# Dealing a projection's matmuls into a recurrence: fewer pieces per preparation, another order of groups, an earlier substitution, a shared tile

## The chip, the cores and the metric

The kernel runs on one core of one Trainium2 chip, as one launch. The metric is device time in microseconds (us). A core has a matmul engine (PE, TensorE), a vector engine (DVE), an activation engine (ACT), GpSimd (POOL) and a queue engine (SP) that issues its DMAs. Each engine works through its own instructions in the order in which they are written down for it; they wait for each other on semaphores.

## The reference

Two transformer blocks on 512 tokens of width 1024, in float32. The first (a hybrid layer: neighbourhood attention, gated linear attention, a convolutional feed-forward network) isn't touched by the change and takes the first 800 us. The second block is:

```
h = rms_norm(x); proj = h @ w_in                      # columns: q, k, v | RWKV columns | gates
attn = windowed_gqa(q, k, v)                           # window of 128, 8 query heads
zr = shift(proj[RWKV columns])                         # r, k, v, decay, rate, gate of the RWKV part
rw = rwkv7_time_mix(zr)                                # 8 heads of 64, forward and backward:
#   state = state * w_t + (state @ a_t) b_t^T + v_t k_t^T;   y_t = state @ r_t
x = x + (gates0 * (attn @ w_up_attn) + gates1 * (rw @ w_up_rwkv)) @ w_out
x = x + relu(rms_norm(x) @ w_ff1)^2 @ w_ff2
x = x + (p @ w_ple) * sigmoid(rms_norm(x) @ w_ple_gate)
```

## The kernel before, in words

The change lies in the method `block2`, in the stage in which the RWKV recurrence is worked out (about 800 to 1242 us of the profiled span). The eight heads are four **parts** of two heads, and the 512 tokens are eight chunks of 64, so that the recurrence becomes matrix work. A part p passes through these functions:

- `prep(p)` (L1060 to L1172): decay, rate and key vectors. PE makes `psw`, `pkn` and `pkr`, ACT and DVE make `kn` (L1096) out of them; here the generator yields the first time. Then, for direction d = 0 and d = 1: `pa`, `pcs` on PE, exponentials on ACT, `kd`, `a`, `u`, `BK`, `Z` on DVE (for d = 1 some of it on POOL), the matmuls `pP` of `Z` and `BK` (L1148), whose masked results `M` (L1151) are stored to DRAM as `scL` (L1157). It yields a second time after d = 0.
- `subst(p)` (L1174): two loads of `scL`, one into `LF` (512 KB, L1178) and one in two halves into `XH` (L1180), then 30 forward-substitution steps on DVE, two small instructions each (`sx` L1186, `XH` L1188), which invert the triangles of 32 rows.
- `finish(p)` (L1191): the result goes over DRAM (`scX`) into `M`, and PE joins the inverted blocks (`pax`, `pt`, `pg`) by way of the tile `AXt`.
- `pre(p)` (L1230), then `chain(p)` (L1258): eight dependent steps over the chunks (`pcb` on PE, `w`, `PV`, `S` on DVE, `W` on ACT), the outputs `pya` and `pyb`, their normalisation (`Z` at L1336, the tile called YT in the code), a yield, and what follows it (`pyt`, `pgt`, `rwd`).

**Pieces.** The projection `h @ w_in` is cut into column groups. Groups 2, 3, 4 are K, R, V of part 0, groups 5, 6, 7 those of part 1, then 8 to 10 and 11 to 13; groups 14 to 29 are the gates (tiles `gt`, stored as `gtd`); "qkv" is the projection for the attention. A group is 24 matmuls of 128x512, "qkv" 288 of 128x256. They need nothing of the recurrence, so they are dealt into it: `queue` (L1485) holds the order of the groups, and `pump(n)` writes the next n pieces into the program at that place (for "qkv" a piece is two matmuls). Groups 2 to 4 are worked out earlier. When a group of K, R or V is done, `cb_rk` and `shift` (L1027 to L1046) write it to `zk`, `zr` or `zv`; the tiles `zk` and `zr` have one buffer each, `zv` two. `need(p)` (L1504) pumps until K, R and V of part p are done. What is left of the queue after chain 3 is written out before the attention.

**Order.** The main loop (L1513 to L1539) writes: `prep(0)`, `need(1)`, `prep(1)`, `subst(0)`, 48 pieces, `finish(0)`, `pre(0)`; and for each p `chain(p)` up to its yield, `subst(p+1)`, `need(p+2)`, `prep(p+2)` up to its first yield, the rest of the chain, `prep(p+2)` up to its second yield, `finish(p+1)`, the rest of `prep(p+2)`, `pre(p+1)`. A scheduler then sets each engine's order; what stands where is shown in the section on the change.

I call **gap p** the time between the end of chain p's `pya`/`pyb` and the first `pcb` of chain p+1.

## Time and profile before

| | us |
|---|---|
| median of 3 runs | 1809.57 (1806.54 to 1810.01) |
| the profiled execution | 1813.19 |
| its span | 1811.4 |
| PE busy in it | 1697.5 |
| start of chain 0 (first `pcb`) | 935.2 |
| gap 0, chain 1, gap 1, chain 2 start at | 970.3, 1013.2, 1052.1, 1117.8 |
| gap 2, chain 3 start at, chain 3 ends at | 1157.1, 1196.8, 1230.0 |
| first matmul of the attention | 1241.85 |

The stages of the table are those that the prediction speaks of. In a timeline row the first number is the start within the span, the second the length, and in square brackets stands how long the engine had been idle and what ended it. The granted clock of PE is told as a share of its upper level of 2.4 GHz; its lower level is 1.2 GHz. A wide "busy" of PE includes matmuls at the lower clock.

### The profile page before, as it was taken

To read this page: it belongs to the slowest core of one execution; us is meant where nothing else is said; L and a number is where in the kernel's file an instruction comes from. 1 tells how busy PE (TensorE), PEld (TensorE's weight loads), DVE (VectorE), ACT (ScalarE), POOL (GpSimd) and SP (SyncE) were. 2 spreads that over 40 slices of the span, in tenths; PEclk is the share of its full clock that TensorE was granted. 3 is DMA by queue.
4 is the path that set the end of the run, shared out by engine and by line. 5 is a ranking of instruction groups with operands and counts; after the bars stand their busy time and mean duration, and the time that the engine had idled before them with its cause. 6 is when DMAs were issued, how large, how long until landed. Compare 5 with 4: busy or idle time off the path is not lost.

```text
span 1811.4 us, 31700 instructions
## 1 busy us (share of the span) xinstructions
PE 1697.5 (94%) x12168; PEld 1427.6 (79%) x12168; DVE 1127.3 (62%) x2375; ACT 780.4 (43%) x1526; POOL 215.7 (12%) x270
## 2 busy tenths in 40 slices
PE   8999998999999999888799898896899999999998
PEld 7888886889988999866676577764478888888887
DVE  5665776787742776867857674765665553355445
ACT  5453456764432445564234232334634442244333
POOL 1100121110000001363321212211000000000000
PEclk9899999999999999999899898897999999999999
DMA  5221223643333334632231212122054333333334
GB/s 170 52 60 48 61 78 113 178 143 99 88 96 97 89 93 139 170 113 62 72 89 45 88 48 67 47 68 70 1 186 146 99 94 99 94 95 98 93 99 129
DMA packets 116087, 170.89 MB, mean 94 GB/s; under 512 B 28839, under 2 KB 43439, under 8 KB 115936
## 3 DMA queue, kind: packets, MB, share of 16 engines
q1 hardware_dynamic: 115936, 168.87, 32.4%
q8 instruction: 96, 1.57, 0.4%
q14 instruction: 55, 0.45, 0.1%
HBM read 155.19 MB, written 13.63 MB: 93 GB/s over the span
## 4 chain that ended last, share of the span: by engine, by line
PE 42%; DVE 8%; DMA 3%; issue 2%; ACT 2%; SPq 1%; POOL 0%; ACTq 0%; DVEq 0%; POOLq 0%
PE ps_w_ff L251 20%; PE ps_w_in L268 5%; PE ps_w_out L251 2%; PE ps_w_ple_gate L251 2%; DMA XH<-scL 1%; PE ps_qkv L1366 1%; PE pP L1148 1%; PE ps_w_up_rwkv L251 1%; DVE sx L1186 1%; PE ps_w_up_attn L251 1%; DVE XH L1188 1%; PE po L1469 1%; DMA LF<-scL 1%; DVE BK L1137 1%; PE pcb L1281 1%
## 5 line engine op out<-in xcount | busy, mean ns | idle before, releaser
L203 DVE TENSOR_TENSOR wl_w_ff<-raw_w_ff,wh_w_ff 128x512 fp32r<-128x512 f32 x128 | 88.2, 689 | 129.8 <-ACT wh_w_ff L202 129.7
L202 ACT ACTIVATE wh_w_ff<-raw_w_ff 128x512 fp32r<-128x512 f32 x128 | 81.0, 632 | 192.2 <-PE ps_w_ff L251 183.4
L202 ACT ACTIVATE wh_w_in<-raw_w_in 128x512 fp32r<-128x512 f32 (+1 forms) x118 | 72.9, 622 | 116.2 <-PE ps_w_in L268 51.3
L203 POOL TENSOR_TENSOR wl_w_in<-raw_w_in,wh_w_in 128x512 fp32r<-128x512 f32 x60 | 81.1, 1354 | 196.7 <-ACT wh_w_in L202 117.4
L202 ACT ACTIVATE wh_w_ffn_in<-raw_w_ffn_in 128x512 fp32r<-128x512 f32 x96 | 60.0, 630 | 99.8 <-PE ps_w_ffn_in L251 88.1
L251 PE MATMUL ps_w_ff<-Yl,wh_w_ff 128*128 128x512 f32 x256 | 100.9, 394 | 0.0
L251 PE MATMUL ps_w_ff<-Yh,wh_w_ff 128*128 128x512 f32 x256 | 100.3, 392 | 0.0
L251 PE MATMUL ps_w_ff<-Yh,wl_w_ff 128*128 128x512 f32 x256 | 99.3, 388 | 0.0
L251 PE MATMUL ps_w_ffn_out<-Y_hi,wl_w_ffn_out 128*128 128x256 f32 (+1 forms) x256 | 83.5, 326 | 3.2 <-DVE wl_w_ffn_out L203 3.1
L251 PE MATMUL ps_w_ffn_out<-Y_hi,wh_w_ffn_out 128*128 128x256 f32 (+1 forms) x256 | 83.6, 326 | 0.0
L251 PE MATMUL ps_w_ffn_out<-Y_lo,wh_w_ffn_out 128*128 128x256 f32 (+1 forms) x256 | 83.3, 326 | 0.0
L203 DVE TENSOR_TENSOR wl_w_ffn_out<-raw_w_ffn_out,wh_w_ffn_out 128x512 fp32r<-128x512 f32 (+1 forms) x72 | 47.4, 663 | 48.2 <-ACT wh_w_ffn_out L202 47.8
L203 DVE TENSOR_TENSOR wl_w_ffn_in<-raw_w_ffn_in,wh_w_ffn_in 128x512 fp32r<-128x512 f32 x96 | 65.7, 689 | 17.0 <-ACT wh_w_ffn_in L202 16.0
L251 PE MATMUL ps_w_ffn_in<-fa_hi,wl_w_ffn_in 128*128 128x258 f32 x352 | 74.3, 285 | 2.0 <-DVE wl_w_ffn_in L203 2.0
L251 PE MATMUL ps_w_ffn_in<-fa_hi,wh_w_ffn_in 128*128 128x258 f32 x352 | 74.0, 284 | 1.7 <-ACT wh_w_ffn_in L202 1.7
L251 PE MATMUL ps_w_ffn_in<-fb_hi,wl_w_ffn_in 128*128 128x258 f32 x352 | 74.0, 284 | 0.2 <-DVE wl_w_ffn_in L203 0.2
L251 PE MATMUL ps_w_ffn_in<-fa_lo,wh_w_ffn_in 128*128 128x258 f32 x352 | 74.2, 284 | 0.0
L251 PE MATMUL ps_w_ffn_in<-fb_hi,wh_w_ffn_in 128*128 128x258 f32 x352 | 74.1, 285 | 0.0
L251 PE MATMUL ps_w_ffn_in<-fb_lo,wh_w_ffn_in 128*128 128x258 f32 x352 | 74.1, 285 | 0.0
L202 ACT ACTIVATE wh_w_ffn_out<-raw_w_ffn_out 128x512 fp32r<-128x512 f32 (+1 forms) x72 | 41.6, 582 | 61.9 <-PE ps_w_ffn_out L251 46.5
L251 PEld LDWEIGHTS ps_w_ffn_in<-fa_hi,wl_w_ffn_in 128*128 128x128 f32 x352 | 56.3, 191 | 2.4 <-DVE wl_w_ffn_in L203 2.4
L251 PEld LDWEIGHTS ps_w_ffn_in<-fa_hi,wh_w_ffn_in 128*128 128x128 f32 x352 | 56.1, 190 | 2.2 <-ACT wh_w_ffn_in L202 1.9
(675 smaller groups left out, 5172.5 us busy)
## 6 DMA issues: line engine op xcount, KB each, us to landing
raw_w_ff<-in_w_ff SPq DMA_DIRECT2D x128, 256.0 KB
raw_w_in<-in_w_in SPq DMA_DIRECT2D x116, 256.0 KB
raw_w_ffn_in<-in_w_ffn_in SPq DMA_DIRECT2D x96, 256.0 KB
raw_w_ffn_out<-in_w_ffn_out SPq DMA_DIRECT2D x40, 256.0 KB
raw_w_o<-in_w_o SPq DMA_DIRECT2D x32, 256.0 KB
raw_w_ffn_out<-in_w_ffn_out SPq DMA_DIRECT2D x32, 192.0 KB
gtd<-gt SPq DMA_DIRECT2D x16, 256.0 KB
g<-gtd SPq DMA_DIRECT2D x16, 256.0 KB
```

The costliest lines, as they stand in the source:

```text
L202: a = nc.scalar.activation(hi, src, AF.Copy)
L203: v = (eng or nc.vector).tensor_tensor(lo, src, hi, ALU.subtract)
L251: mm = nc.tensor.matmul(ps[si][:ncol, :s1 - s0], a[:, k, :], bk[:, s0:s1], start=(ks == k0 and k == 0 and pi == 0), stop=(ks + k == kend - ...
L268: nc.tensor.matmul(pw[:ncol, 0, :n], a[:, k, :], b[kk // 4][:, kk % 4, :n], start=(kk == 0 and pi == 0), stop=(kk == kend - 1 and pi == 2))
L1137: nc.vector.scalar_tensor_tensor(BK[H[e], :, O[e]], perm(a[H[e]], 64), -0.5, perm(iE[H[e]], 64), ALU.mult, ALU.mult)
L1148: nc.tensor.matmul(pps[e][:, i, :], BK[H[e], 4 * hf + i, :], Z[hf][H[e], i, :], start=True, stop=True)
L1186: nc.vector.tensor_tensor(sv, XH[:, 0:k, t:t + 1].to_broadcast([128, k, n]), LF[:, t % 2, t // 2:t // 2 + 1, t + 1:32].to_broadcast([128, ...
L1188: nc.vector.tensor_tensor(XH[:, 0:k, t + 1:32], XH[:, 0:k, t + 1:32], sv, ALU.add)
L1281: nc.tensor.matmul(pu[O[e], d, :], M[e][O[e], d, cd[d], 0:64], w[O[e], d, :], start=True, stop=True)
L1366: nc.tensor.matmul(pq[i][:, :256], l, r[:, k - ks, :], start=(k == 0 and n == 0 and i % 2 == 0), stop=(k == 7 and n == 2 and i % 2 == 1))
L1469: nc.tensor.matmul(po[own[g]], KVv[:, b0 + b, 128 + 64 * g:192 + 64 * g], PT[n % 2][:, g, b, :], start=b == 0, stop=b == nk - 1)
```

## The change

The order of the main loop becomes one loop over p (below). For p = 0, `need(5, 6)` pumps K and R of part 1 only, `subst(0)` follows the first third of `prep(1)`, and `finish(0)` comes between the two directions of `prep(1)`, with 24 pieces where it had 12; the block of 48 pieces is gone. The preparations of parts 2 and 3 deal 32 pieces each where they had 69. The queue names other groups first. `zk` has two buffers. The tile `AXt` of `finish`, which had a buffer of its own, now takes the buffer of `LF` (half of it), and that there is only one such buffer stays.

```diff
-                dct, nm, bf = ((Kt, "zk", 1), (R, "zr", 1), (V, "zv", 2))[j]
+                dct, nm, bf = ((Kt, "zk", 2), (R, "zr", 1), (V, "zv", 2))[j]
...
-            pump(4)
+            pump(2 if p else 4)
...
-            pump(8)
+            pump(4 if p else 8)
...
-                    pump((18, 15)[d] if len(Z) == 1 else 6)
+                    pump((8 if p else (18, 15)[d]) if len(Z) == 1 else 2 if p else 6)
...
-                    pump(4 if len(BKT) == 1 else 2)
+                    pump((4 if len(BKT) == 1 else 2) // (2 if p else 1))
...
-            AXt = rk.tile([128, 2, 8, 32], F32, tag="AX", name=f"AX{p}")
-            pump(12 if p == 0 else 6)
+            AXt = rk.tile([128, 2, 16, 32], F32, tag="LF", name=f"AX{p}").rearrange("p h m t -> p (h m t)")[:, :512].rearrange("p (d c t) -> p d c t", d=2, c=8)
+            pump(24 if p == 0 else 6)
...
-        queue = [5, 6, 7] + list(range(14, 19)) + [8, 9, 10] + list(range(19, 23)) + [11, 12, 13, 23, "qkv"] + list(range(24, 30))
+        queue = [5, 7, 14, 6, 15, 16, 8, 9, 17, 10, 18, 11, 12, 19, 13, "qkv"] + list(range(20, 30))
...
-        def need(p):
-            while not set(range(3 * p + 2, 3 * p + 5)) <= done | {2, 3, 4}:
+        def need(*gs):
+            while not set(gs) <= done | {2, 3, 4}:
                 pump(1)
...
         run(prep(0))
-        need(1)
-        run(prep(1))
-        XH = subst(0, pr[0][4])
-        pump(48)
-        finish(0, XH, pr[0][3])
-        x = pre(0, *pr[0][:4])
+        tail = iter(())
         for p in range(4):
-            ch = chain(p, *pr[p][:4], *x)
-            run(ch, 1)
-            nx = None
+            if p:
+                XH = subst(p, pr[p][4])
+            nx = iter(())
             if p < 3:
-                XH = subst(p + 1, pr[p + 1][4])
-            if p < 2:
-                need(p + 2)
-                nx = prep(p + 2)
+                need(3 * p + 5, 3 * p + 6)
+                nx = prep(p + 1)
                 run(nx, 1)
-            run(ch)
-            if p < 3:
-                if nx:
-                    run(nx, 1)
-                finish(p + 1, XH, pr[p + 1][3])
-                if nx:
-                    run(nx)
-                x = pre(p + 1, *pr[p + 1][:4])
+            if not p:
+                XH = subst(p, pr[p][4])
+            run(tail)
+            run(nx, 1)
+            finish(p, XH, pr[p][3])
+            run(nx)
+            need(3 * p + 4)
+            x = pre(p, *pr[p][:4])
+            tail = chain(p, *pr[p][:4], *x)
+            run(tail, 1)
+        run(tail)
```

How many pieces stand ahead of certain places in PE's order ("qkv" counted as two matmuls a piece):

| pieces written before | before | after |
|---|---|---|
| chain 0 starts / ends | 253 / 303 | 238 / 308 |
| chain 1 starts / ends | 360 / 423 | 333 / 383 |
| chain 2 starts / ends | 528 / 578 | 444 / 496 |
| chain 3 starts / ends | 639 / 703 | 567 / 629 |

The first place is DVE around the first step of substitution 0. A name like `kd10` is tile `kd` of part 1, direction 0; `sx01` is step 1 of part 0. Before:

```order
L1096 TENSOR_TENSOR kn1_10024<-kn1_10024,pkr1_10056 128x512
L1119 TENSOR_SCALAR kd10_10078<-a10_10068,kah_82,ka1_81 128x512
...
L1143 TENSOR_TENSOR Z101_10132<-zr1_9902,Er_9644 128x4x64
L1056 TENSOR_TENSOR gt1_10220<-ps_w_in_2_15_10106,rsh_75 128x512
L1186 TENSOR_TENSOR sx01_10314<-XH0_10310,LF0_10309 128x30
L1188 TENSOR_TENSOR XH0_10310<-XH0_10310,sx01_10314 128x30
L1186 TENSOR_TENSOR sx02_10317<-XH0_10310,LF0_10309 128x29
```

In the changed kernel the same place reads:

```order
L1096 TENSOR_TENSOR kn1_10065<-kn1_10065,pkr1_10085 128x512
L1186 TENSOR_TENSOR sx01_10096<-XH0_10092,LF0_10091 128x30
L1188 TENSOR_TENSOR XH0_10092<-XH0_10092,sx01_10096 128x30
...
L1186 TENSOR_TENSOR sx06_10111<-XH0_10092,LF0_10091 128x75
L1056 TENSOR_TENSOR gt1_10303<-ps_w_in_2_15_10041,rsh_75 128x512
L1188 TENSOR_TENSOR XH0_10092<-XH0_10092,sx06_10111 128x3x25
L1119 TENSOR_SCALAR kd10_10202<-a10_10192,kah_82,ka1_81 128x512
L1186 TENSOR_TENSOR sx07_10114<-XH0_10092,LF0_10091 128x96
```

The whole DVE work of direction 0 of preparation 1 (twelve instructions) has moved from ahead of `sx01` to behind its sixth step, and so has the tile `gt1`.

The second place is SP's queue around the load of `LF` for part 1; in the brackets stand the engines and DMA queues whose semaphores the load waits for. Before:

```order
L1203 DMA M01_9736<-scX0_10488 16x16x32 [waits DMAHW3_49]
L1178 DMA LF1_11103<-scL1_10065 128x1x1024 [waits DMAHW4_49]
L1180 DMA XH1_11104<-scL1_10065 64x512 [waits DMAHW5_49]
L1180 DMA XH1_11104<-scL1_10065 64x512 [waits DMAHW6_49]
L211 DMA raw_w_in_2_2555904_11235<-in_w_in_2 128x512 [waits DMAHW7_49,Pool_49]
```

And in the changed kernel:

```order
L1180 DMA XH1_11019<-scL1_10189 64x512 [waits DMAHW6_49,DMAHW2_49]
L1180 DMA XH1_11019<-scL1_10189 64x512 [waits DMAHW7_49,DMAHW3_49]
L211 DMA raw_w_in_2_1441792_11462<-in_w_in_2 128x512 [waits DMAHW4_49,Pool_49]
L1178 DMA LF1_11018<-scL1_10189 128x1x1024 [waits DMAHW5_49,DVE_49,PE_49]
L211 DMA raw_w_in_2_1507328_11634<-in_w_in_2 128x512 [waits Pool_49]
```

The load waits for DVE and PE now, since its buffer is that of `AX0`, which the matmuls `pg` of `finish(0)` (L1226) read last. `LF1`'s first reader, `sx11`, stands on DVE behind `w01`, the `w` of chain 0's step 1, in the changed kernel; before, it stood ahead of the chain's first step.

The third place is DVE at the first step of substitution 2, which runs beside chain 1; `w12` is the `w` of step 2 of chain 1. Before:

```order
L1277 TENSOR_TENSOR w12_11824<-pcb12_11819,W01_11685 128x128
...
L1277 TENSOR_TENSOR w13_11858<-pcb13_11853,W01_11685 128x128
L1042 TENSOR_TENSOR zs11_11881<-zt0_9641 128x512
L1186 TENSOR_TENSOR sx21_12126<-XH2_12122,LF2_12121 128x30
L1044 SCALAR_TENSOR_TENSOR zk3_11880<-zs11_11881,mu2_78,zk3_11880 128x512
```

And in the changed kernel:

```order
L1277 TENSOR_TENSOR w11_11648<-pcb11_11643,W01_11542 128x128
L1088 TENSOR_SCALAR knr3_12095<-pkn3_12090 128x8
...
L1277 TENSOR_TENSOR w12_11676<-pcb12_11671,W01_11542 128x128
L1096 TENSOR_TENSOR kn3_12084<-kn3_12084,pkr3_12104 128x512
L1186 TENSOR_TENSOR sx21_11978<-XH2_11974,LF2_11973 128x30
```

The step stands one chain step earlier, and the first third of preparation 3, which before came after chain 1 (`kn3` stood behind the last step of substitution 2), is now done inside chain 1; the first `Z` of part 3 stands behind step 21 of substitution 2. Substitution 3's first step, which stood behind one `w` of chain 2, now stands behind three.

## Rows read from the trace of the kernel before

**Rows 1.** page, section 1: busy us (share of the span) xinstructions, whole kernel

```profile
PE 1697.5 (94%) x12168; PEld 1427.6 (79%) x12168; DVE 1127.3 (62%) x2375; ACT 780.4 (43%) x1526; POOL 215.7 (12%) x270
```

**Rows 2.** busy time per engine by stretch; columns as its first line says

```profile
core 0: us, PE busy (x) PEld busy (x) DVE busy (x) ACT busy (x) POOL busy (x), PEclk, DMA share, GB/s
871.70:911.90 40.20, 34.94 (x166) 27.99 (x167) 35.14 (x80) 10.48 (x18) 14.67 (x12) 0.82 0.23 59
911.90:935.20 23.30, 22.25 (x329) 18.10 (x328) 9.70 (x14) 7.20 (x12) 3.98 (x4) 0.91 0.44 119
935.20:970.30 35.10, 34.34 (x448) 24.31 (x447) 27.73 (x94) 12.39 (x24) 6.51 (x5) 0.96 0.15 42
970.30:1013.20 42.90, 38.76 (x464) 29.78 (x457) 30.62 (x59) 17.33 (x29) 10.81 (x9) 0.92 0.25 65
1013.20:1052.10 38.90, 33.25 (x425) 22.04 (x424) 24.64 (x76) 8.12 (x18) 7.85 (x7) 0.91 0.26 77
1052.10:1117.80 65.70, 61.22 (x601) 51.11 (x600) 41.70 (x84) 23.83 (x43) 16.06 (x13) 0.90 0.22 56
1117.80:1157.10 39.30, 32.96 (x467) 27.49 (x466) 21.46 (x84) 9.15 (x21) 6.87 (x6) 0.87 0.16 51
```

**Rows 3.** DVE timeline: start us, us, line op out<-in, [idle before <-releaser]

```profile
871.71 0.19 DVE L1186 TENSOR_TENSOR sx<-XH,LF 128x30 f32<-128x30 f32 x1 [2.94 <-issue]
...
932.11 0.68 DVE L1016 COPY M<-pg 32x512 f32<-32x512 f32 x1 [2.94 <-PE pg L1226]
...
934.72 0.19 DVE L1186 TENSOR_TENSOR sx<-XH,LF 128x30 f32<-128x30 f32 x1
...
939.35 0.29 DVE L1277 TENSOR_TENSOR w<-pcb,W 128x128 f32<-128x128 f32 x1 [0.19 <-PE pcb L1275]
```

**Rows 4.** SP timeline (DMA issues): start us, us, line, transfer

```profile
856.69 0.59 SPq L1178 DMA_DIRECT2D LF<-scL  x1
...
919.46 0.57 SPq L1178 DMA_DIRECT2D LF<-scL  x1
```

**Rows 5.** busy by stretch, columns as in rows 2, of 10 us

```profile
860.00:870.00 10.00, 7.62 (x42) 5.51 (x40) 8.38 (x12) 2.82 (x6) 3.02 (x2) 0.97 0.38 127
1130.00:1140.00 10.00, 9.51 (x72) 7.92 (x72) 4.97 (x24) 1.70 (x5) 1.34 (x1) 0.55 0.10 28
```

**Rows 6.** DVE timeline, the second half of prep 2, between chains 0 and 1

```profile
1004.64 1.29 DVE L1151 TENSOR_TENSOR M<-pP,cst 128x512 f32<-128x512 f32 x2 [0.52 <-PE pP L1148]
1007.90 1.29 DVE L1151 TENSOR_TENSOR M<-pP,cst 128x512 f32<-128x512 f32 x2 [0.41 <-PE pP L1148]
```

**Rows 7.** DVE timeline inside chain 1 and chain 2

```profile
1020.73 0.28 DVE L1277 TENSOR_TENSOR w<-pcb,W 128x128 f32<-128x128 f32 x1
...
1024.43 0.29 DVE L1277 TENSOR_TENSOR w<-pcb,W 128x128 f32<-128x128 f32 x1
...
1030.52 1.23 DVE L1186 TENSOR_TENSOR sx<-XH,LF 128x30 f32<-128x30 f32 x1 [5.20 <-DMA XH<-scL]
...
1129.77 0.19 DVE L1186 TENSOR_TENSOR sx<-XH,LF 128x30 f32<-128x30 f32 x1 [7.72 <-DMA XH<-scL]
```

**Rows 8.** DVE timeline: first Z after chain 0; BK and Z of prep 3

```profile
984.58 0.42 DVE L1142 TENSOR_TENSOR Z<-kn,Er 128x256 f32<-128x256 f32 x1 [0.81 <-PE pyt L1340]
...
1075.44 0.67 DVE L1137 SCALAR_TENSOR_TENSOR BK<-a,iEr 64x512 f32<-64x512 f32 x1
...
1078.04 0.43 DVE L1142 TENSOR_TENSOR Z<-kn,Er 128x256 f32<-128x256 f32 x1
...
1101.42 1.67 DVE L1137 SCALAR_TENSOR_TENSOR BK<-a,iEr 64x512 f32<-64x512 f32 x1
```

**Rows 9.** PE timeline: first matmuls of prep 3

```profile
1054.51 1.89 PE L1073 MATMUL psw<-W,TW 65*128 65x256 f32 x8
```

**Rows 10.** PE timeline after chain 3: first and last of 34 pieces

```profile
1229.89 0.50 PE L268 MATMUL ps_w_in<-ha_lo,wh_w_in 128*128 128x512 f32 x1
...
1237.64 0.39 PE L268 MATMUL ps_w_in<-hb_lo,wh_w_in 128*128 128x512 f32 x1
```

## The prediction

> **What bounds the kernel now.** I read the page's first section first: PE is busy for 94% of the span [rows 1]. So time can come only from PE's idle time, from the stretches in which its clock is low, or from less matmul work; and the change leaves the matmuls as they are and only deals them elsewhere. Then I cut the RWKV stage at its own marks, the starts and ends of the chains, and asked for busy time by stretch [rows 2]. The reader is to compare PE's busy column with the stretch: chain 0 has 34.34 of 35.1 us, gap 1 61.22 of 65.7, but chain 1 only 33.25 of 38.9 and chain 2 32.96 of 39.3. The timeline of DVE says why: in chain 1 and chain 2 DVE stands for 5.20 and 7.72 us at the first step of a substitution until its load has landed [rows 7], and the chain's own steps stand behind that step in DVE's order. Substitution 0, on the other side, is nearly a pure DVE stretch: 35.14 of 40.2 us [rows 2].
>
> A piece costs (1237.64 - 1229.89)/33 = 0.235 us at the full clock, where 34 of them run back to back [rows 10]. The question for each edit is therefore whether the pieces that it takes away stood on the path (then the stage gets shorter by 0.235 each) or filled a time in which PE would have waited. What is taken away is paid at the end: 74 more pieces stand behind chain 3 (629 against 703, from the order), where nothing hides them.
>
> **The change part by part.** All terms are differences to the profiled execution of before, whose 1813.19 us lie 3.6 over the median of the three runs; I add the sum to the median, 1809.57.
>
> *Up to chain 0.* Substitution 0 stands right behind `kn1` now. That doesn't start it earlier: its load was issued at 856.69, and the first step ran at 871.71, after DVE had waited 2.94 us [rows 3, 4]. What DVE did meanwhile, direction 0 of preparation 1, fills most of 860 to 870, 8.38 us [rows 5]; in the new order it stands behind step 6, so DVE waits at the first step instead, and PE's `pP` of that direction waits for DVE. From 871.7 on DVE then has 35.14 + 8.38 = 43.5 us of work, against the 40.2 that the stretch lasted: 3.3 us later if DVE never waits, 8.4 if its waits stay as they were. PE has 15 pieces (3.5 us) less before chain 0, but the first third of preparation 2 now stands there too, 3 sets of 8 matmuls at 1.89 us, 5.7 us, in a stretch in which PE is busy for 22.25 of 23.3 [rows 2, 9]. I take +5, with 0 (PE's smaller load decides, and the load lands sooner) and +11 (8.4 plus the 2.2 that PE has more) as ends.
>
> BK may be dearer than this. The same instruction took 0.67 us at one place and 1.67 at another [rows 8], and POOL splits weights all along this stretch (14.67 us busy, [rows 2]); four of them at the long price would be 4 us more, which the end of +11 nearly holds. The Trainium skill (SBUF — State Buffer, section "SBUF: two separate sides") says that DVE and GpSimd share one pair of ports as an exclusive lock, held for a whole instruction, where a DVE instruction with two inputs in SBUF meets a GpSimd one that reads SBUF. By that rule all of direction 0's products, moved to a place where POOL is busier, would take the long price, and the sum below would be 4 us higher. The two prices in the trace agree with it.
>
> *Chain 0 and LF.* LF(1) was issued at 919.46 [rows 4], long before its first use at 934.72 [rows 3]. With AXt in LF's buffer it has to wait for `pg` of part 0. DVE's copy of `pg` starts at 932.11 [rows 3], 3.1 us before chain 0 begins. From issue to first use LF(0) took 871.71 - 856.69 = 15.0 us, so LF(1) is there 11.9 us after chain 0's start. DVE comes to `sx11` after `w01`, at 939.64 or 4.4 us after the start [rows 3], and stands there for 7.5 us with chain 0's steps behind it. Behind LF(1) on SP stand weights of group 11 only, which the next 26 pieces (6 us) don't need. Chain 0 also gets 20 more pieces (4.7 us) while PE has no room (34.34 of 35.1). If pieces and stall hide each other wholly, chain 0 grows by the larger, 7.5; if not at all, by 12.2; if DVE finds the load landed, by 4.7. I take +7.5. LF(3) waits for `pg` in the same way, but its `scL` comes last anyway, and the same for LF(2): nothing.
>
> *Gap 0* loses 32 pieces, 7.5 us. It is a relay between PE, ACT and DVE, in which pieces mostly fill PE's waits. DVE's waits that stand right behind shortened deals are those for `pP`, 0.52 and 0.41 [rows 6]: I take -0.9 out of 0 to -7.5.
>
> *Chain 1.* The first step of substitution 2 stands behind two `w` instead of three, so DVE arrives 1024.43 - 1020.73 = 3.7 us sooner [rows 7] at a load that lands when it did: the wait of 5.20 becomes 8.9. The first third of preparation 3 goes into the chain as well, and 13 pieces (3.1 us) go out; these cancel against each other. +3.7, ends 0 and +6.
>
> *Gap 1* is the large gain. Before, the first third of preparation 3 had to pass in it: its first Z came 1078.04 - 1052.10 = 25.9 us after the chain, against 984.58 - 970.30 = 14.3 in gap 0 [rows 2, 8]. Now it is done in chain 1, as that of part 2 was in chain 0. PE's work in the gap falls by 5.7 (the same three sets) and by 44 pieces (10.3): 61.22 - 16.0 = 45.2 us. At gap 0's busy share of 38.76/42.9 = 0.903 [rows 2] that takes 50.1 us: -15.6. Ends: -11.6 (only the earlier Z) and -21 (every removed matmul, and all of PE's idle 4.5).
>
> *Chain 2.* Substitution 3's first step stands behind three `w` where it stood behind one. Two steps are 7.4 us, the wait was 7.72: it goes, and with it PE's idle 39.3 - 32.96 = 6.3 [rows 2, 7]. What is late next is the chain's own step. -6.3, ends -3 and -6.3. Gap 2 and chain 3 get 10 pieces more and 2 fewer: nothing, at most +2.4. The second `zk` is in the sum already: it is what lets K of part 3 be worked out so early.
>
> *Behind chain 3* stand 74 more pieces: +17.4 us, with no other work beside them but the last normalisation.
>
> Sum: 5 + 7.5 - 0.9 + 3.7 - 15.6 - 6.3 + 17.4 = +10.8, so 1820.4 us. The likeliest case's own range is 1814 to 1827.
>
> **The rivals.**
> *A, faster: PE's load decides.* If pieces stood on the path nearly everywhere, moving them costs nothing, and only PE's idle time counts: chain 2's 6.3, chain 1's 5.6, gap 1's 4.5 go, and the 5 us up to chain 0 come. 1809.6 - 16.4 + 5 = 1798. For it: PE's 94%, and gap 1. Against it: LF(1) and the later arrival of work at substitution 0 are waits in which PE has little to do.
>
> *B, no change.* As A, but the new LF(1) wait stays (+7.5), and chain 1's idle isn't won: 1809.6 - 10.8 + 5 + 7.5 = 1811. This is also the case in which the early substitution does not do what its place says, since the load isn't there any sooner, and the rest balances.
>
> *C, slower still: the clock.* After the 7.72 us wait the granted clock was 0.55 in the ten us from 1130, PE busy for 9.51 of them [rows 5]: 0.45 x 9.51 = 4.3 us of work lost to the lower level. The forecast has three long waits of PE that are new or longer (first step of substitution 0, LF(1), substitution 2) and loses one. If each new one costs 4.3 more, two net are 8.6: 1829. It decides from the point at which PE stands still for most of a wait, as it did in chain 2; if the 20 extra pieces fall into the wait, it doesn't. The Trainium skill (TensorE: Matmul & The Clock Gate, section "HAM oscillation — how this bites in real kernels") says likewise that a pause for data sends the array back to its lower clock and is paid for a second time after it; the row agrees.
>
> **How the numbers follow.** Forecast 0.42, A 0.25, B 0.17, C 0.16. This kernel's runs can tell about 0.2%, 3.6 us, from no change: faster means under 1806, slower over 1813.2. A counts as faster (0.25), and of B's 0.17 I give 0.04 to faster, 0.11 to same and 0.02 to slower. The forecast gives 0.03 to same, C all to slower. Faster 0.29, same 0.14, slower 0.57. The range of 1800 to 1830 leaves out about half of A below and a third of C above, 2 in 10 in all.
>
> **What would show it.** Right: in the profile of the changed kernel DVE's first `sx` waits for over 8 us and runs at 868 to 872; chain 0's first `pcb` comes at 935 to 946; LF(1) is issued after DVE's copy of `pg`, and one `sx` in chain 0 waits 5 to 8 us for it; gap 1 takes 48 to 54 us, chain 2 about 33; some 115 pieces run dense after chain 3, about 28 us. Wrong: if gap 0 or the stretch up to chain 0 shrinks by the pieces taken out (then A), if `sx11` doesn't wait, or if PE's clock after the new waits stays at its upper level while the sum still comes out longer.

## The result and the profile after

The changed kernel takes 1832.33 us (median of 4, 1827.19 to 1836.32) against 1808.05 us for the kernel before: a ratio of 1.0136, interval 1.0104 to 1.0168, some 24 us slower. The direction was forecast; the time lies 12 us over the 1820.4 and 2 over the range's upper end.

One slip has to be put right first. The section on the change and the prediction speak of shorter deals in the preparations of parts 2 and 3. The condition in the code is `if p`, so the preparation of part 1 deals less as well; and the kernels `d1_deals_back` and `after_old_deals` below, whose expectations name parts 2 and 3, put pieces back in all three.

The profiled execution after is the fastest of its runs (1827.19 us, span 1825.4), and that of before (1813.19) is slower than all four runs of its median. The two traces therefore differ by 14.0 us only; the other 10 of the 24 us lie between executions and are in no trace. The trace after shows this, first the page's line of busy time:

```profile
PE 1698.7 (93%) x12168; PEld 1428.1 (78%) x12168; DVE 1123.9 (62%) x2375; ACT 783.8 (43%) x1528; POOL 217.5 (12%) x270
```

PE is as busy as before, 1698.7 against 1697.5 [rows 1], in a span that is 14.0 longer: it is idle for 12.8 us more. Next comes busy time by stage, with the columns of [rows 2]: from the first `psw` of part 0's second half to chain 0, then chain 0, gap 0, chain 1, gap 1, chain 2, gap 2, chain 3, and what lies between chain 3 and the last piece ahead of the attention.

```profile
798.00:939.33 141.33, 120.38 (x823) 92.71 (x824) 88.36 (x164) 53.15 (x86) 40.46 (x33) 0.87 0.24 69
939.33:981.50 42.17, 33.12 (x429) 22.42 (x425) 29.30 (x93) 6.85 (x16) 10.18 (x8) 0.92 0.23 71
981.50:1025.70 44.20, 35.06 (x414) 25.50 (x416) 32.11 (x58) 15.84 (x26) 7.84 (x7) 0.88 0.17 39
1025.70:1066.30 40.60, 35.88 (x483) 26.72 (x479) 24.39 (x85) 12.62 (x24) 5.22 (x5) 0.96 0.18 55
1066.30:1122.80 56.50, 50.38 (x521) 43.65 (x519) 35.52 (x66) 18.24 (x32) 14.19 (x12) 0.78 0.21 51
1122.80:1153.80 31.00, 29.96 (x467) 25.26 (x465) 22.41 (x83) 8.23 (x19) 5.57 (x4) 0.96 0.18 57
1153.80:1196.80 43.00, 35.96 (x387) 27.71 (x389) 33.77 (x113) 17.93 (x38) 7.83 (x7) 0.88 0.26 71
1196.80:1227.60 30.80, 30.63 (x427) 20.66 (x422) 11.21 (x37) 7.15 (x16) 6.49 (x5) 1.00 0.23 70
1227.60:1256.30 28.70, 28.40 (x121) 22.19 (x122) 10.27 (x18) 12.99 (x19) 9.56 (x7) 1.00 0.40 121
```

The stages that [rows 2] doesn't hold read as follows in the kernel before:

```profile
802.00:935.20 133.20, 114.90 (x799) 89.87 (x800) 89.56 (x159) 48.36 (x79) 43.12 (x35) 0.88 0.30 84
1157.10:1196.80 39.70, 34.05 (x388) 27.61 (x390) 30.53 (x100) 14.35 (x34) 6.88 (x6) 0.83 0.19 49
1196.80:1230.00 33.20, 32.29 (x430) 21.61 (x427) 13.67 (x47) 8.91 (x18) 6.49 (x5) 1.00 0.26 81
1230.00:1241.80 11.80, 10.96 (x47) 8.27 (x48) 8.56 (x15) 7.18 (x10) 1.30 (x1) 1.00 0.29 82
```

Stage by stage that is (after less before, with the prediction's term):

| | start to chain 0 | chain 0 | gap 0 | chain 1 | gap 1 | chain 2 | gap 2 | chain 3 | behind it |
|---|---|---|---|---|---|---|---|---|---|
| measured | +8.1 | +7.1 | +1.3 | +1.7 | -9.2 | -8.3 | +3.3 | -2.4 | +16.9 |
| predicted | +5 | +7.5 | -0.9 | +3.7 | -15.6 | -6.3 | 0 | 0 | +17.4 |

The sum is +18.5 where +10.8 was forecast; the stretch ahead of these stages, where the change edits nothing, was 4.0 shorter in this execution, and what follows them 0.5. The lines that answer to [rows 3, 4] (DVE's and PE's timeline with the idle time before an instruction and what ended it, and SP's issues of `LF`):

```profile
866.93 0.19 DVE L1186 TENSOR_TENSOR sx<-XH,LF 128x30 f32<-128x30 f32 x1 [7.93 <-DMA XH<-scL]
...
938.52 0.68 DVE L1016 COPY M<-pg 32x512 f32<-32x512 f32 x1 [0.31 <-PE pg L1226]
...
943.45 0.27 DVE L1277 TENSOR_TENSOR w<-pcb,W 128x128 f32<-128x128 f32 x1
...
952.16 0.19 DVE L1186 TENSOR_TENSOR sx<-XH,LF 128x30 f32<-128x30 f32 x1 [8.44 <-DMA LF<-scL]
```

```profile
954.64 0.69 PE L1275 MATMUL pcb<-PV,Z 64*64 64x64 f32 x8 [8.25 <-DVE PV L1296]
```

```profile
853.12 0.59 SPq L1178 DMA_DIRECT2D LF<-scL  x1
...
938.45 0.58 SPq L1178 DMA_DIRECT2D LF<-scL  x1
```

`LF` of part 1 is issued at 938.45, with the copy of `pg`, and DVE stands for it for 8.44 us with chain 0 behind it; PE stands still for 8.25. In the stretch behind it, from 948 to 952, where the load is still under way, the DMA engines' mean busy share (second figure from the end) is 0.13, that of 2 of the 16:

```profile
948.00:952.00 4.00, 0.00 (x0) 0.00 (x0) 0.00 (x0) 0.00 (x0) 0.00 (x0) 0.92 0.13 52
```

The first step of substitution 2, in chain 1, waits for its load for 4.37 us, where it waited for 5.20 before [rows 7]:

```profile
1041.87 0.19 DVE L1186 TENSOR_TENSOR sx<-XH,LF 128x30 f32<-128x30 f32 x1 [4.37 <-DMA XH<-scL]
```

In gap 1 two of DVE's products `BK` of the second direction take the long time of [rows 8], and PE has to wait for them ahead of the first `pP`: 2.40 us, where it waited 0.74 for that direction in the kernel before. The lines are DVE after, PE after, PE before:

```profile
1093.10 1.74 DVE L1137 SCALAR_TENSOR_TENSOR BK<-a,iEr 64x512 f32<-64x512 f32 x1
...
1096.53 1.67 DVE L1137 SCALAR_TENSOR_TENSOR BK<-a,iEr 64x512 f32<-64x512 f32 x1
```

```profile
1094.99 2.04 PE L1148 MATMUL pP<-Z,BK 64*128 64x128 f32 x8 [2.40 <-DVE BK L1137]
```

```profile
1104.07 1.16 PE L1148 MATMUL pP<-Z,BK 64*128 64x128 f32 x16 [0.74 <-DVE Z L1142]
```

Behind that wait PE's granted clock (the third figure from the end) reads, in the changed kernel:

```profile
1094.80:1108.30 13.50, 12.94 (x67) 10.57 (x69) 7.49 (x10) 1.76 (x3) 2.85 (x2) 0.50 0.07 10
1101.00:1104.00 3.00, 3.00 (x28) 2.68 (x27) 0.52 (x2) 0.58 (x1) 0.00 (x0) 0.50 0.00 0
1104.00:1107.00 3.00, 3.00 (x8) 1.86 (x9) 1.58 (x3) 0.14 (x1) 0.00 (x0) 0.50 0.11 16
...
1110.00:1113.00 3.00, 3.00 (x82) 2.70 (x81) 0.68 (x1) 0.44 (x1) 0.00 (x0) 1.00 0.73 220
...
1118.00:1121.00 3.00, 3.00 (x59) 2.94 (x58) 0.68 (x1) 0.09 (x1) 1.32 (x2) 0.50 0.02 5
```

From 1101 to 1107 and from 1118 to 1121 PE works without a pause and yet at 0.50 of the upper level, which is 1.2 GHz. The first of these low stretches began with the wait of 2.40 us; between them the clock was at its upper level, and the second began, at 1115, with no pause ahead of it. Over the gap the clock is 0.78, where it was 0.90.

### The profile page after: what moved, and what is told of

Its sections match the earlier page's. It is cut to its first block, busy times and chain, and to the rows that moved or that the text cites. A ratio compares the mean times of both kernels' runs of the same rounds, so it can differ in the third digit from the quotient of the medians.

```text
span 1825.4 us, 31702 instructions
## 1 busy us (share of the span) xinstructions
PE 1698.7 (93%) x12168; PEld 1428.1 (78%) x12168; DVE 1123.9 (62%) x2375; ACT 783.8 (43%) x1528; POOL 217.5 (12%) x270
## 4 chain that ended last, share of the span: by engine, by line
PE 43%; DVE 9%; DMA 3%; issue 2%; ACT 2%; POOL 0%; SPq 0%; DVEq 0%; ACTq 0%; POOLq 0%
PE ps_w_ff L251 19%; PE ps_w_in L268 6%; PE ps_w_out L251 2%; PE ps_w_ple_gate L251 2%; PE ps_qkv L1366 1%; DMA XH<-scL 1%; PE pP L1148 1%; DVE XH L1188 1%; DVE sx L1186 1%; PE ps_w_up_rwkv L251 1%; PE ps_w_up_attn L251 1%; DVE BK L1137 1%; PE po L1469 1%; DMA LF<-scL 1%; PE pcb L1281 1%
```

## The experiments

Ratios are to the kernel before, run on the same chip; in brackets stands the 95% interval. A ratio of 0.001 is 1.8 us. They fall into four questions.

**What does the load of LF cost?** First AXt gets another buffer in the changed kernel, so that the load needn't wait for `pg`; then the reverse, AXt in LF's buffer in the kernel before. Code lines are shortened here and below; "..." stands for the rest of a line.

```diff
-            AXt = rk.tile([128, 2, 16, 32], F32, tag="LF", ...
+            AXt = rl.tile([128, 2, 8, 64], F32, tag="W0", ...
```

> The changed kernel, with AXt in the (then dead) buffer of W0 instead of that of LF, so that the load of LF(1) no longer waits for pg. Theory 1 (the shared buffer costs a stall of the whole chain): the 8.44 us wait of DVE at the first step of substitution 1 goes, chain 0 takes about 35 us instead of 42.2, and the time falls by 7 to 8 us, to about 1824.5 (1832.3 before this edit). Rival (PE's load decides, the wait only moves idle time elsewhere): chain 0 gets shorter, gap 0 longer, and the time stays within 2 us of 1832.

1829.76 us, 1.0100 [1.0071, 1.0130]. Chain 0 takes 33.2 us instead of 42.2, PE idle for 1.5 instead of 9.0, but most of it is lost again: the stretch up to chain 0 is 2.4 us longer, chain 1 3.6 and the stretch from chain 3 to the attention 4.5. The interval overlaps that of the changed kernel (1.0104 to 1.0168), so this run alone doesn't decide between the two theories.

> The kernel before, with only AXt put into the buffer of LF, as in the change. Theory 1 (the shared buffer makes LF(1) wait for pg, and the chain's first steps stand behind its first use): DVE waits some 10 us at the first step of substitution 1, and the kernel is 7 to 12 us slower than before, 1817 to 1822. Rival (PE has pieces enough to fill that wait): within 2 us of before.

1820.60 us, 1.0051 [1.0033, 1.0069]: +9.2 us for this edit alone, and the wait is there:

```profile
943.17 0.19 DVE L1186 TENSOR_TENSOR sx<-XH,LF 128x30 f32<-128x30 f32 x1 [6.16 <-DMA LF<-scL]
```

Then the load itself: 512 KB, whose access pattern has 2 as its outermost size, are loaded as two DMAs of 64 rows each, in either kernel.

```diff
-  dma_start(LF, AP(fl, [[0, 2], [1024, 64], [1, 1024]]))
+  for h in range(2):
+      dma_start(LF[64 * h:64 * h + 64], AP(fl, [[1024, 64], [1, 1024]]))
```

> The changed kernel, with the load of LF written as two loads of 64 partitions each, whose pattern has 64 rows as its outermost dimension, where the one load had 2. Theory 4 (the load is slow because it runs on few DMA engines, and its landing sets the waits at the first steps of substitutions 0, 1 and 2): it lands about 5 us after its issue instead of 13 to 15, the waits of 7.9, 8.4 and about 4 us shrink to 2 or less, and the time falls by 10 to 18 us, to 1814 to 1822. Rival (the order of issue on SP and the other load, XH, decide): the waits stay, and the time within 2 us of 1832.

1819.94 us, 1.0044 [1.0029, 1.0059].

> The kernel before, with the load of LF split in the same way. Theory 4: DVE's waits of 2.9, 5.2 and 7.7 us at the first steps of substitutions 0, 2 and 3 shrink to 2 or less, chains 1 and 2 get about 5 us shorter each, and the kernel is 7 to 13 us faster than before, 1797 to 1803. Rival (XH decides): within 2 us of before.

1798.48 us, 0.9935 [0.9912, 0.9957]: faster than both kernels. In either trace no first step of a substitution waits for its load any more, and the same bytes come much sooner. In the changed kernel LF of part 1 took 952.16 - 938.45 = 13.7 us from issue to first use; with the two halves, issued from 934.98 on, the first step runs without a wait (SP's and DVE's timelines):

```profile
934.98 1.09 SPq L1179 DMA_DIRECT2D LF<-scL  x2
```

```profile
941.79 0.17 DVE L1187 TENSOR_TENSOR sx<-XH,LF 128x30 f32<-128x30 f32 x1
```

At most 6.8 us, then. The Trainium skill (DMA: Bandwidth & Descriptors, section "Why a DMA increments its semaphore by 16 and not by 1") says that a DMA is spread over as many engines as divide its slowest dimension on both sides, up to 16; by that rule an outermost size of 2 gets two of them and one of 64 gets sixteen. The two runs agree, with 13.7 us against at most 6.8, and so does the DMA share of 0.13 above. In the kernel before the split also takes the waits of [rows 7]: chain 1 takes 31.2 us (38.9 before), chain 2 30.1 (39.3). So the waits for loads in the substitutions were worth some 12 us in the kernel before and 12 (by the medians) to 17 (by the ratios) in the changed one. They tell the two apart by little: with the split in both, the changed order is still 21.5 us slower.

Forcing the first step of substitution 0 behind direction 0 of preparation 1 (a copy of one element of its `Z` into the step's tile) was inconclusive.

> The changed kernel, with the first step of substitution 0 forced behind direction 0 of preparation 1 on DVE, as in the kernel before (a copy of one element makes it depend on that direction's last Z). Theory 1 (the step at the head of DVE's queue blocks direction 0, and PE waits for it at the lower clock): PE's idle time between the landing of the load and the end of substitution 0 falls from 14.2 to about 6 us, its granted clock there rises from 0.74 to over 0.8, and the time falls by 6 to 9 us, to 1823 to 1826. Rival (the load's landing and DVE's total work decide): substitution 0 ends when it did, and the time stays within 2 us of 1832.

1831.01 us, 1.0114 [1.0091, 1.0138]. The stretch up to chain 0 shrinks from 141.3 to 134.1, gap 0 grows from 44.2 to 51.2 at a clock of 0.63; the time is that of the changed kernel within the intervals.

**Is it the deals?** Pieces were put back into the changed kernel's preparations: those of the second direction, all of them, those of part 1; and the short deals of parts 2 and 3 were set into the kernel before.

```diff
-                    pump((8 if p else (18, 15)[d]) if len(Z) == 1 else 2 if p else 6)
+                    pump(((8, 15) if p else (18, 15))[d] if len(Z) == 1 else 2 if p and d == 0 else 6)
```

> The changed kernel, with the deals of direction 1 of preparations 2 and 3 as they were before (15 and 6 pieces ahead of the two pP, where the changed kernel has 8 and 2): 22 pieces more in gaps 0 and 1, 22 fewer (5.2 us) behind chain 3. Theory 2 (these pieces filled DVE's long stretch of direction 1, and without them PE stands still and then runs the rest of the gap at the lower clock): the granted clock in gap 1 rises from 0.78 to about 0.9, gap 1 gets no longer or shorter, the tail 5 us shorter, and the time falls by 5 to 9 us. Rival (a piece costs the same wherever it stands on a PE that is busy): the gaps grow by what the tail loses, and the time stays within 2 us of 1832.

1850.05 us, 1.0221 [1.0194, 1.0248]: slower, against the theory.

> The changed kernel with all deals of preparations 2 and 3 as before (69 pieces each in place of 32), the rest as changed. Theory 2 (the pieces fill waits): 74 pieces leave the tail, 17.4 us, the gaps grow by 7 to 12 us, and the kernel is 5 to 10 us faster than the changed one, 1822 to 1827. Theory 5 (what counts is where wide pieces stand in the relay, and these deals stand ahead of it): the tail shrinks by 17 us, the gaps grow by as much or more, and the time stays within 5 us of 1832 or gets longer, as it did when the deals of one direction alone were restored.

1847.89 us, 1.0207 [1.0182, 1.0232]; only 10 of the 115 pieces behind chain 3 leave that place, and gap 0 takes 59.6 us at a clock of 0.71. Gap 1 alone does what the theory said; its line is shown below, with the prediction's step.

> The changed kernel, with the deals of preparation 1 alone as before (69 pieces in place of 32), those of preparations 2 and 3 short as changed. The condition in the changed code shortens preparation 1 too. Theory 7 (the 15 us by which the time up to chain 0 is longer in the changed order come from PE standing still, and then running at the lower clock, beside substitution 0, since preparation 1 brings too few pieces): the stretch up to chain 0 keeps its length with 19 pieces more in it, its clock rises from 0.87 to over 0.9, and the time falls by 3 to 8 us. Rival (restored deals lengthen what they stand in, as in the two kernels in which deals of all preparations were restored, at 13 and 15 us): slower by 5 us or more.

1839.66 us, 1.0158 [1.0134, 1.0181].

> The kernel before, with only the deals of preparations 2 and 3 cut to 32 pieces as in the change; nothing else. 74 pieces (17.4 us) move behind chain 3. Theory 2 (the pieces filled waits): gaps 0 and 1 shrink by much less than 17.4 us together and their granted clock falls, so the kernel is 6 to 12 us slower than before, 1814 to 1820. Rival (pieces stand on the path in the gaps): the gaps shrink by what the tail gains, and the time stays within 2 us of 1808.

1817.73 us, 1.0039 [1.0023, 1.0055]. With AXt in LF's buffer as well:

> The kernel before, with both edits that cost time alone: AXt in LF's buffer (+9 us alone) and the deals of preparations 2 and 3 cut to 32 pieces (+7 us alone). Theory 6 (the two costs stand in different places, chain 0 and gap 1, and add up; the new order of the groups and of the loop is worth some 8 us more): 14 to 18 us slower than before, 1823 to 1828. Rival (they share one cause, the clock of the gaps, and most of the change's 24 us comes from the order): 8 to 11 us slower.

1821.40 us, 1.0062 [1.0040, 1.0083]: 11 us, where the two add up to 16; the intervals don't tell these apart. And the short deals with the split load:

> The kernel before with the load of LF split and the deals of preparations 2 and 3 cut to 32. Theory 2 (short deals leave the relay of gap 1 without wide pieces): 5 to 10 us slower than with the split alone, 1804 to 1808. Rival (the deals only cost where a load made the chains wait): within 2 us of 1798.

1798.56 us, 0.9931 [0.9908, 0.9953], the same as the split alone. So the short deals cost nothing that can be told once the loads are in time, and long ones in the changed order make it worse.

**Is it the clock?** Matmuls of full width whose results are overwritten were added, in the changed kernel ahead of `pP` and `pyt` (80 in all), then 36 inside the relay `pt`, `pg`, `pv`, `pk` of parts 1 and 2, there and in the kernel before with the split load. These runs do more work than the kernel asks for.

```diff
+            if 1 <= p <= 2:
+                for x in (pt1, pg2_):        # and likewise for pv, pk
+                    for _ in range(3):
+                        nc.tensor.matmul(x, h_hi[0][:, 0, 0:128], h_hi[0][:, 1, :S], start=True, stop=True)
```

> The changed kernel, with 80 matmuls of 128x512 added whose results are overwritten at once: 8 ahead of each of the four pP deals of preparations 2 and 3, and 8 ahead of the transposes pyt of chains 0 and 1. They cost PE 18.8 us at the full clock and move nothing else. Theory 3 (PE's short waits at the start of a gap drop the clock, and the relay of small matmuls that follows then runs at the lower level): the granted clock of gaps 0 and 1 rises from 0.88 and 0.78 to over 0.9, and the kernel gets faster by 3 to 8 us in spite of the added work, or at the least no slower. Rival (PE's work decides in the gaps): slower by 10 to 19 us.

1839.34 us, 1.0151 [1.0126, 1.0176]. PE's idle time in gap 0 falls from 9.1 to 4.0, the clock only rises from 0.88 to 0.89: the wait of 3.23 us ahead of `pyt` is gone, but the clock falls some us later without one. In gap 1 the wait ahead of `pP` stayed (2.35 us) and the clock is 0.80, so for that gap the run tests nothing.

> The changed kernel, with 36 matmuls of 128x512 added (8.5 us of PE at the full clock) whose results are overwritten at once: 3 ahead of each of pt, pg, pv and pk of parts 1 and 2, inside the relay of narrow matmuls that ends gaps 0 and 1. Theory 5 (the clock falls, or stays down, while PE runs narrow matmuls of 32 and 64 rows back to back without wide ones between them, busy or not): the granted clock of gaps 0 and 1 rises from 0.88 and 0.78 to over 0.9, and the kernel is 0 to 8 us faster than the changed kernel in spite of the added work, 1824 to 1833. Rival (only idle time lowers the clock, and PE has no room in the relay): the clock stays, and the kernel is 6 to 12 us slower, 1838 to 1845.

1835.21 us, 1.0149 [1.0122, 1.0176]: no gain. Gap 1 is at 0.78 as it was, and gap 0 falls from 0.88 to 0.81, with a low stretch of 6.7 us among the added matmuls.

> The kernel before with the load of LF split, with the same 36 matmuls added in the relays of gaps 0 and 1. Theory 5: the granted clock of gaps 0 and 1 rises from 0.80 and 0.84 to over 0.9, and the time stays at 1798 or falls by up to 8 us. Rival: the clock stays and the time rises by 6 to 12 us.

1795.18 us, 0.9925 [0.9903, 0.9948], the lowest median here, though its interval holds the split's 0.9935. 36 wide matmuls at 0.235 are 8.5 us of work, and it is no slower than without them: gap 0 goes from 52.0 to 50.7 us with the clock from 0.80 to 0.93, gap 1 from 74.6 to 72.5 with 0.84 to 0.88. The same place of gap 0, in the relay, without and then with them:

```profile
998.00:1011.60 13.60, 13.60 (x212) 10.96 (x215) 3.93 (x6) 2.44 (x5) 0.00 (x0) 0.50 0.34 88
```

```profile
998.00:1012.00 14.00, 14.00 (x290) 10.76 (x288) 4.32 (x7) 3.24 (x6) 0.12 (x1) 1.00 0.35 85
```

In this order the clock thus fell inside the relay, a run mostly of matmuls of 32 to 64 rows, without a pause, and didn't fall there with wide matmuls among them; each is one profiled execution. A longer low stretch is one of the short deals in the kernel before. It began with a wait of PE of 2.98 us ahead of `pP`, and then, busy by 6 us, PE first, the granted clock third from the end:

```profile
1087.00:1093.00 6.00, 6.00 (x54) 5.01 (x53) 2.60 (x5) 0.00 (x0) 0.00 (x0) 0.50 0.00 0
1093.00:1099.00 6.00, 6.00 (x43) 4.01 (x42) 0.98 (x2) 2.08 (x5) 0.00 (x0) 0.50 0.15 22
1099.00:1105.00 6.00, 6.00 (x87) 5.71 (x87) 2.52 (x4) 1.86 (x4) 0.00 (x0) 0.50 0.41 101
1105.00:1111.00 6.00, 6.00 (x67) 5.02 (x65) 4.74 (x6) 0.94 (x3) 5.80 (x4) 0.50 0.01 3
```

24 us without a further pause at the lower level. In the changed order the filling didn't help, so there the relay's narrow matmuls aren't shown as the cause; what is shown there is the wait ahead of the low stretch.

**Which part of the order?** With the load split and AXt in W0's buffer the changed kernel is back at 1.0038; with the deals of part 1 and substitution 0 put back as well it doesn't come any lower.

> The changed kernel with both mends: LF loaded in two halves, and AXt in the buffer of W0. Theory 1 and 4 together: with a load that lands in 5 us the shared buffer costs little, so little is added: 1814 to 1819 against 1820 with the split alone. Rival (the two waits add up): 6 us faster than the split alone, 1812 to 1814. What stays above 1810 is then the deals and the order, not the loads.

1816.86 us, 1.0038 [1.0019, 1.0056].

> The changed kernel with the load of LF split, AXt in the buffer of W0, the first step of substitution 0 behind direction 0 of preparation 1, and preparation 1 with its old deals; what stays of the change is the order of the groups, the loop, the second zk and the short deals of preparations 2 and 3. Theory 6: what stays is worth little, 1803 to 1810. Rival (the order itself costs, through the clock of the stretch up to chain 0 and of the gaps): 1813 to 1820, as with the first two mends alone (1817).

1817.89 us, 1.0044 [1.0025, 1.0063]. What is left is the loop, the queue of groups and the second `zk`. The last two kernels cross them: the old queue and one `zk` in the mended changed kernel, the new queue and two `zk` in the mended kernel before. The short deals are in all four, in the old loop without those of part 1; AXt lies in W0's buffer in all but the first, old loop with old queue, where it has its own.

```diff
-        queue = [5, 6, 7] + list(range(14, 19)) + [8, 9, 10] + list(range(19, 23)) + [11, 12, 13, 23, "qkv"] + list(range(24, 30))
+        queue = [5, 7, 14, 6, 15, 16, 8, 9, 17, 10, 18, 11, 12, 19, 13, "qkv"] + list(range(20, 30))
```

> The changed kernel with LF loaded as two halves and AXt in W0's buffer (measured 1.0038 of before), in which the queue of groups and the single zk buffer of the kernel before are put back; the loop and the short deals stay. Theory 8, the queue costs (K and R of part 2 are pumped so early that the first third of preparation 2 stands ahead of chain 0, and the column group 6 behind a gate group): 0.994 to 0.998, and the stretch from psw(0) to chain 0 shrinks from about 138 to under 131 us. Theory 9, the loop costs (substitution 0 and finish 0 lie inside preparation 1): 1.002 to 1.006, the stretch stays at 135 to 140 us.

1798.90 us, 0.9952 [0.9934, 0.9969].

> The kernel before with LF loaded as two halves and the short deals in parts 2 and 3 (measured 0.9931 of before), to which the changed kernel's queue and the doubled zk are added (AXt sits in W0's buffer, to make room for zk); the old loop stays. Theory 8, the queue costs: 1.000 to 1.004, with 290 pieces ahead of chain 0 by the order and a stretch from psw(0) to chain 0 of 133 us or more. Theory 9, the loop costs: 0.992 to 0.996, the stretch at 126 to 130 us.

1822.25 us, 1.0076 [1.0060, 1.0093].

| load split, short deals | old queue, one zk | new queue, two zk |
|---|---|---|
| old loop | 0.9931 [0.9908, 0.9953] | 1.0076 [1.0060, 1.0093] |
| new loop | 0.9952 [0.9934, 0.9969] | 1.0038 [1.0019, 1.0056] |

The queue (with its `zk`) costs 1.45% in the old loop and 0.86% in the new one; the loop costs nothing that can be told with the old queue, and gains 0.4% with the new one. The clean pair is the second, since AXt's place differs in the first. In the traces the cost shows in three places. Busy time up to chain 0, in chain 0 and behind chain 3 (up to the first matmul `paS` of the attention), first with the old loop and the old queue:

```profile
801.50:927.80 126.30, 109.69 (x799) 84.92 (x801) 89.60 (x157) 48.16 (x79) 43.21 (x35) 0.93 0.33 89
927.80:962.10 34.30, 33.65 (x454) 23.92 (x450) 28.08 (x95) 12.40 (x25) 6.52 (x5) 1.00 0.14 42
...
1211.30:1244.50 33.20, 22.03 (x97) 16.60 (x95) 16.45 (x27) 16.26 (x25) 5.49 (x12) 0.85 0.36 105
```

and with the old loop and the new queue:

```profile
797.00:933.60 136.60, 121.12 (x837) 94.46 (x839) 91.54 (x160) 48.68 (x80) 46.38 (x37) 0.91 0.31 86
933.60:972.50 38.90, 33.64 (x424) 24.67 (x418) 30.02 (x107) 11.78 (x23) 5.34 (x5) 0.78 0.10 31
...
1222.30:1263.00 40.70, 29.53 (x129) 22.81 (x129) 18.61 (x29) 19.31 (x30) 10.16 (x16) 0.89 0.37 116
```

Up to chain 0 it is 10.3 us longer. The new queue names group 6, which part 1 needs, behind 7 and 14, so `need(1)` has to bring the pieces written to 96 where 72 did; in PE's order 290 stand ahead of chain 0 against 253, and 37 x 0.235 = 8.7 us. Of these 37, 24 are that group more; why the other 13 stand there too isn't shown. Chain 0 is left with 22 pieces where it had 52, and it isn't shorter for that: it is 4.6 us longer, with PE idle for 5.3 us instead of 0.7, between the chain's own steps, and at a clock of 0.78. And 102 pieces stand behind chain 3 instead of 71: 31 x 0.235 = 7.3 of the 7.5 us there. What lies between chain 0 and the end of chain 3 differs by 0.6 us, so AXt's place costs little in parts 1 to 3, whose `finish` lies there. Up to the V of part 3 the new queue asks for 360 pieces, the old one for 432. The new loop with the two queues shows the same in smaller size (old queue first):

```profile
797.70:933.90 136.20, 118.38 (x800) 92.75 (x804) 87.15 (x164) 50.67 (x81) 39.20 (x32) 0.85 0.27 76
933.90:965.50 31.60, 31.55 (x439) 21.59 (x433) 27.91 (x90) 9.01 (x20) 8.18 (x6) 0.99 0.20 60
```

```profile
801.60:943.50 141.90, 127.02 (x838) 98.89 (x840) 92.46 (x171) 52.77 (x85) 40.93 (x34) 0.86 0.28 76
943.50:981.40 37.90, 32.99 (x422) 22.47 (x416) 28.42 (x96) 7.68 (x18) 9.03 (x8) 0.86 0.22 64
```

30 pieces more ahead of chain 0 (258 against 228) are 7.1 us, 5.7 show; chain 0 has 4.9 us of idle time that the old queue doesn't have.

## Why the prediction was right in direction and wrong in size

- *Chain 0 and LF, +7.5:* right. The wait was 8.44 us (7.5 forecast), chain 0 grew by 7.1, and the edit alone cost the kernel before 9.2.
- *Up to chain 0, +5:* right in kind. The first step waits 7.93 us and runs at 866.93, which is 68.9 us into the stage where it was 69.7 before: no earlier, as forecast. Chain 0 starts 8.1 us later by its stage, inside the bound of 11. The dearer `BK` that the prediction feared here didn't come: of the four of direction 0 one took the long time (1.75 us), and two had before (1.78 and 1.75).
- *Chain 2, -6.3, and behind chain 3, +17.4:* right: -8.3 and +16.9; the 8.3 holds the idle time (6.3 to 1.0) and the clock (0.87 to 0.96).
- *Gap 0, -0.9:* it came out at +1.3. Its 32 pieces went and PE's busy time fell from 38.76 to 35.06 us, but the idle time rose from 4.1 to 9.1: here the pieces had filled waits.
- *Chain 1, +3.7:* it came out at +1.7, and not for the reason given: the wait was to grow from 5.20 to 8.9 us, and it was 4.37.
- *Gap 1, -15.6:* this is the step that failed, with 6.4 of the 7.7 us by which the stages' sum misses the forecast. It took PE's 45.2 us of work at gap 0's busy share of 0.903, and left the clock as it was. The share was about right (50.38 of 56.5 is 0.89), but the work took 50.38 us, since the clock fell to 0.78: 5.2 of the 6.4 us are the longer busy time, 1.3 idle. In the trace the longest low stretch of the gap begins with PE's wait of 2.40 us for `BK`, for which the prediction had no term. Two runs bear it out. In the kernel before with the short deals alone, gap 1 holds 75 matmuls less and is hardly shorter than the 65.70 us of before: PE waits 2.98 us ahead of the first `pP`, there of direction 0, and the clock is 0.74 instead of 0.90. In the changed kernel with all the old deals the waits ahead of `pP` are 1.32 and 0.71 us in place of 2.42 and 2.40 (direction 0 and 1), and the clock is 0.92, with 85 matmuls more in 60.9 us instead of 56.5:

```profile
1055.50:1120.93 65.43, 59.48 (x526) 49.22 (x527) 41.24 (x79) 20.82 (x36) 13.06 (x10) 0.74 0.17 41
```

```profile
1084.86:1145.75 60.89, 57.09 (x606) 49.25 (x607) 41.55 (x73) 26.28 (x46) 15.09 (x13) 0.92 0.21 55
```

With the deals of the second direction alone (`d1_deals_back`) its wait stays, at 2.54 us, and the clock is 0.79, so the number of pieces at that place isn't all of it. In the prediction's terms this is rival C, a wait and then the lower clock, at a place that C didn't name; its 1829 is nearest to the measured 1832, in part by luck, since C counted waits that the forecast had elsewhere. And the second low stretch of the gap, from 1115, has no wait ahead of it, which C didn't say.
- *Gap 2, 0:* +3.3, of which 1.9 is busy time, for the ten pieces more (2.4 at most, as forecast), and 1.4 idle.
- *The accounting by pieces.* The prediction counted pieces by stage and put them down to shorter deals. The runs say otherwise for the kernel as a whole: deals put back make it slower, for what gap 1 gains gap 0 loses, and the deals cut in the kernel before cost 0.4% only as long as the loads are late. With the loads mended, most of the loss goes with the queue of groups (and its `zk`), to which the prediction gave no term.
- *Rivals A and B* fell: the pieces taken out did not pay for themselves.
- *The size as a whole.* The time misses the forecast by 12 us. In the profiled pair the stages miss by 7.7, and 4.5 come back outside of them; the other 9 us lie in how far each profiled execution is from its median, and no trace shows what they are.

In how far the queue alone makes up the +24 us of the unmended kernel is inferred: it was taken out of the mended one (+0.86% there, +1.07% for loop and queue together, some 19 us). What is left of the 24, some 5 us, fits the wait for LF, 1.0136 to 1.0100 when it is taken away, but those intervals overlap. Open stays whether the second `zk` has a share in the queue's cost, since the two were changed together, why PE's filled relay recovers the clock in one order and not in the other, and what makes PE reach `pP` ahead of `BK` in gap 1 by so much.

## What to carry to other kernels

Fill work that is dealt into a dependent chain has two orders: how many pieces go where, and which group a `need` has to pull through the queue first; count in the final order what stands ahead of the first chain and behind the last, at the price of a piece, for every queue that you try. Look at the outermost size of a DMA's access pattern where a step waits for a load, before moving the step: splitting one load was worth 12 us, nearly as much as the order of the groups (0.86 to 1.45%, 16 to 26 us), and a tile that shares the buffer moves the load's issue to its last reader. Forecast a stage by its clock as well as its busy share, and ask of every stage that loses fill work what PE will stand and wait for.

## What the hardware showed that was not expected

The granted clock can stay at 1.2 GHz while PE is busy for every microsecond: 24 us in a run mostly of narrow matmuls, behind a wait of 3 us. In the relay of another kernel it fell without a wait just ahead of it, for 13.6 us, and 36 wide matmuls in that relay gave back all they cost; in the changed order they did not. And a load of 512 KB whose outermost size is 2 took 13.7 us from issue to use, while two of 256 KB with 64 rows were there in at most 6.8.
